# Products with their low-part passes last, joined seams, scan tables on GpSimd and grouped transposes in a neighbourhood-attention / S5 / FFN block

## The chip, the cores and the metric

One core of a Trainium2 chip runs the whole kernel. The metric is the device time of one execution in microseconds. The program is written with a tile framework whose list scheduler puts each engine's instructions into one fixed order before the run; on the chip every engine works its list off in that order, waiting on semaphores for the others.

## The reference

One layer over 2048 latent tokens (a grid 64 wide) and 256 context tokens, width 1024, all in fp32:

```
n  = modulate(rmsnorm(x)), n_ctx = modulate(rmsnorm(ctx))
q,k,v,u,gate_a,gate_s = split(n @ w_in)
a  = neighbourhood_attention(rope(q), rope(k), v, k_ctx, v_ctx, bias)
s  = glu(gelu(S5_forward(u) + S5_backward(u) + d * u))
h  = x + g1 * ((sigmoid(gate_a) * (a @ w_ba) + sigmoid(gate_s) * (s @ w_bs)) @ w_out)
h  = h + g2 * swiglu(modulate(rmsnorm(h)))     # hidden width 2816
out = rmsnorm(h)
```

S5 is a complex diagonal scan: 32 groups of 64 states in 2 directions. Here it runs over chunks of 8 tokens, 32 context chunks and 256 latent ones (288 columns).

## The kernel before

**Products.** Every dense fp32 product is made of fp32r passes. `split` (L68) makes of a tensor a high part on ScalarE (L70, `whi`) and a remainder on VectorE (L71, `wlo`). `mm3` (L89) then issues three matmuls for each 128-row slice k: high x high, and the two mixed ones. So the low part of the first slice of a weight is wanted by the second or third matmul of a product. `piece` (L79) loads 512 KB of weights over the SP queue and splits them; `cols` (L96) has the weights stationary, `rows` (L111) and the FFN's second product have them moving. `prod` (L1062) has its own copy of the three passes for the FFN's first product, a Strassen-like scheme of seven 256-column products per tile.

**Stages.** `norm_u` normalises and projects u; then `s5` and `in_proj` (the q, k, v and gate columns, four blocks of 512 tokens) are laid over each other: `in_proj` has a low priority and fills TensorE beside the scan, later beside `attention`; `merge` follows, and the FFN takes the second half of the time. The normalised tokens of a block are eight tiles `n` of a ring of twelve, reloaded from memory for blocks 1 to 3 (L357).

**The scan.** `s5` runs over 4 quarters and 2 sub-blocks (8 rounds). Each round loads u over the POOL queue into `ut` (L651), transposes it on TensorE (L658 to L661: four transposes and one ScalarE copy for each of four groups, the context chunk transposed twice because it stands at both ends of a row of `ug`), and builds small matrices. Then come four passes (2 pairs of groups x 2 directions), 32 in the kernel. A pass makes a table of complex exponentials `er`, `ei` of 288 columns by doubling (L734 to L744): copies of the first 32 columns and four rounds of two scalings on ScalarE (L741, L742) and two multiply-adds on VectorE (L743, L744), each round needing the one before. Then it multiplies the driven states `pv` (PSUM, L750) by the table (L757 to L760), scans (L762), multiplies back and writes `h` (L765 to L772). The tables have two buffers. At the start of block 1 of `in_proj`, `biases` puts the attention biases together on GpSimd (L442, L443) and stores them.

The scheduler sets the order by priorities and its own estimate of times, so a change in one stage also shifts what stands beside it.

Of the kernel before, what the change touches and what calls it, by code (L numbers as in the profile page):

```python
# [18 lines left out]
P = 128  # L19
# [33 lines left out]
class Kernel:  # L53
# [35 lines left out]
    def mm3(self, ps, l, r, first, last):  # L89

        mm = self.nc.tensor.matmul
        mm(ps, l[0], r[0], start=first, stop=False)  # L92
        mm(ps, l[0], r[1], start=False, stop=False)  # L93
        mm(ps, l[1], r[0], start=False, stop=last)  # L94

    def cols(self, pool, src, kt, c0, n, ops, tag="ps"):  # L96

        nm = 8 // kt  # L100
        for c in range(n):
            w = self.piece(src, 0, c0 + c, kt)
            for m in range(nm):
                sl = slice(m * P, (m + 1) * P)
                for i, (nt, f) in enumerate(ops):
                    ps = pool.tile([P, nt], F32, name=tag)
                    for k in range(kt):
                        self.mm3(ps, (w[0][:, k, sl], w[1][:, k, sl]), f(k), k == 0, k == kt - 1)
                    yield c * nm + m, i, ps

    def rows(self, pool, src, c, ops, tag="ps"):  # L111


        w = [self.piece(src, r, c, 4) for r in range(2)]
        for i in range(0, len(ops), 2):
            ps = pool.tile([P, 2, 256], F32, name=tag)
            for j in range(2):
                for k in range(KD):
                    self.mm3(ps[:, j], ops[i + j](k), (w[k // 4][0][:, k % 4], w[k // 4][1][:, k % 4]), k == 0, k == KD - 1)
            yield i, ps  # L120
# [163 lines left out]
    def norm_u(self, ring, s5p):  # L284

        nc, I = self.nc, self.I
        with ExitStack() as ctx:
# [19 lines left out]
            def u(ops, t0, i0, i1):  # L307
                for c in range(2):
                    for i in range(i0, i1, 2):
                        ps = pm.tile([P, 2, 256], F32, name="ps")  # L310
                        for j in range(2):
                            for k in range(KD):
                                w = wu[c * 2 + k // 4]
                                self.mm3(ps[:, j], ops[i + j](k), (w[0][:, k % 4], w[1][:, k % 4]), k == 0, k == KD - 1)
# [35 lines left out]
    def in_proj(self, ring, ev, pm, nt, nct):  # L350
        nc, I = self.nc, self.I
        V = nc.vector
        for b in range(NB):
# [16 lines left out]
            def qk(c0, ops, isk):  # L370
                for jj, i, ps in self.cols(pm, I["w_qk"], KD, c0, 4, ops):
# [50 lines left out]
            for gi in range(2):  # L422
                for m, _, ps in self.cols(pm, I["w_gate"], KD, gi * 8, 8, [lat]):
# [205 lines left out]
    def s5(self):  # L629
        nc, I = self.nc, self.I  # L630
        V = nc.vector
        with ExitStack() as ctx:
# [7 lines left out]
            for q in range(4):  # L640
                yn = [bp.tile([P, SC, 8, 16], F32, name=f"yn{cb}") for cb in range(2)]
                for sb in range(4 // NQ):
# [84 lines left out]
                    for p0 in range(0, NQ, 2):  # L727
                        hst = {}
                        for p in (p0, p0 + 1):
                            for d in range(2):  # L730
                                pr = d * 16 + pr0 + p
                                er = pp.tile([P, SEQC], F32, name="er")
                                ei = pp.tile([P, SEQC], F32, name="ei")
                                nc.scalar.copy(er[:, 0:32], self.eb[:, 0, :, pr])  # L734
                                nc.scalar.copy(ei[:, 0:32], self.eb[:, 1, :, pr])
                                for i, m in enumerate((32, 64, 128, 256)):
                                    w = min(m, SEQC - m)
                                    zr, zi, zn = (self.zz[:, i, x, pr:pr + 1] for x in range(3))
                                    ea = pp.tile([P, P], F32, name="ea", bufs=1)
                                    eb = pp.tile([P, P], F32, name="eb", bufs=1)  # L740
# [278 lines left out]
    def ffn_in(self, ch, b, X, pm, os, tp, up):  # L1019
# [77 lines left out]
    def ffn(self, xs_, os, xp, tp, pm, first):  # L1097
        nc, I = self.nc, self.I
        V = nc.vector
        with ExitStack() as ctx:  # L1100
# [13 lines left out]
            for b in range(NB):  # L1114
# [4 lines left out]
                for g, (p0, p1) in enumerate(groups):  # L1119
# [39 lines left out]
                    def product(c, m2, j, w):  # L1159
                        js = slice(j * P, (j + 1) * P)  # L1160
                        for m in range(2):
                            zh, zl = zs[m2, m]
                            self.mm3(pos[j], (zh[:, js], zl[:, js]), (w[0][:, m], w[1][:, m]), m2 == p0 and m == 0, m2 == p1 - 1 and m == 1)
# [183 lines left out]
```

## Time and profile before

| | us |
|---|---|
| median of 3 runs | 3233.86 (3228.43 to 3234.4) |
| profiled execution, device time | 3233.39 |
| its span in the profile | 3231.6 |
| TensorE matmul busy in the span | 3119.2 |
| VectorE / ScalarE / GpSimd busy | 2348.4 / 1570.3 / 898.9 |

A wait is listed under the instruction that waited and the one that released it. TensorE's instructions overlap, so the distance between starts, not the duration of one, tells what a matmul costs in a dense stretch. The granted clock is 1.00 at 2.4 GHz and 0.5 at 1.2 GHz.

### The profile page before, as it was taken

What the parts mean: (1) busy time and instruction counts of PE and PEld (TensorE: products, weight loads), DVE (VectorE), ACT (ScalarE), POOL (GpSimd) and SP (SyncE); (2) the same over time, 40 slices, a digit from 0 to 9 for tenths busy, and PEclk for the clock granted to TensorE, in tenths of its full rate; (3) what the DMA queues carried; (4) which work ended last, traced back from release to release, by engine and by line L of the source; (5) the groups of instructions that cost most, each with busy time, mean ns of one, the idle gap of its engine ahead of it and who ended that gap; (6) DMA issues with size and microseconds to landing.
All of it is one profiled execution on the core that took longest, in us unless ns stands there. A gap on an engine that the chain in (4) does not pass through costs nothing.

```text
span 3231.6 us, 54283 instructions
## 1 busy us (share of the span) xinstructions
PE 3119.2 (97%) x20600; PEld 2727.7 (84%) x20600; DVE 2348.4 (73%) x4153; ACT 1570.3 (49%) x2746; POOL 898.9 (28%) x856
## 2 busy tenths in 40 slices
PE   7999978999999998999999999999999999999998
PEld 5987766787787778788888988888989898989988
DVE  6689787897753565665657867887858966897766
ACT  4445434454355555555554444445535543554534
POOL 2000052000223232323300544742242423341243
PEclk9999989999999999999999999999999999999999
DMA  8545567454776897987847434434344434443332
GB/s 321 186 125 172 166 194 241 163 163 140 228 211 193 268 259 213 277 238 220 254 130 269 139 126 146 141 131 147 122 136 132 150 111 131 141 147 131 112 111 101
DMA packets 212853, 564.27 MB, mean 175 GB/s; under 512 B 31785, under 2 KB 63657, under 8 KB 212593
## 3 DMA queue, kind: packets, MB, share of 16 engines
q1 hardware_dynamic: 155008, 437.48, 41.2%
q0 software_dynamic: 28032, 87.64, 10.0%
q10 hardware_dynamic: 29552, 35.70, 3.2%
q8 instruction: 162, 2.65, 0.3%
q14 instruction: 99, 0.80, 0.1%
HBM read 446.95 MB, written 111.61 MB: 173 GB/s over the span
## 4 chain that ended last, share of the span: by engine, by line
PE 79%; DVE 9%; DMA 6%; issue 3%; POOL 1%; ACT 1%; SPq 0%; ACTq 0%; DVEq 0%; POOLq 0%
PE ps L92 15%; PE ps L94 15%; PE ps L93 15%; PE ps L1068 8%; PE ps L1066 8%; PE ps L1067 8%; PE o L924 3%; DVE wlo L71 3%; PE w L884 2%; PE w L905 1%; DMA raw<-in_w_qk 1%; PE pv L750 1%; PE c L886 1%; PE c L907 1%; DVE n L1130 1%
## 5 line engine op out<-in xcount | busy, mean ns | idle before, releaser
L71 DVE TENSOR_TENSOR wlo<-raw,whi 128x1024 fp32r<-128x1024 f32 (+1 forms) x522 | 688.0, 1325 | 324.6 <-ACT whi L70 323.1
L70 ACT CAST whi<-raw 128x1024 fp32r<-128x1024 f32 (+1 forms) x522 | 508.3, 976 | 519.6 <-PE ps L94 185.8
L1066 PE MATMUL ps<-X,whi 128*128 128x256 f32 x2464 | 693.4, 284 | 13.2 <-DVE u L1078 8.4
L1068 PE MATMUL ps<-X,wlo 128*128 128x256 f32 x2464 | 692.4, 284 | 11.9 <-DVE wlo L71 11.7
L1067 PE MATMUL ps<-X,whi 128*128 128x256 f32 x2464 | 689.9, 283 | 0.0
L1066 PEld LDWEIGHTS ps<-X,whi 128*128 128x128 f32 x2464 | 471.2, 191 | 17.9 <-DVE u L1078 11.7
L1068 PEld LDWEIGHTS ps<-X,wlo 128*128 128x128 f32 x2464 | 470.5, 191 | 15.1 <-DVE wlo L71 14.9
L1067 PEld LDWEIGHTS ps<-X,whi 128*128 128x128 f32 x2464 | 471.3, 191 | 0.5
L92 PE MATMUL ps<-n,whi 128*128 128x512 f32 (+1 forms) x800 | 318.2, 398 | 10.3 <-ACT t L382 6.7
L93 PE MATMUL ps<-n,whi 128*128 128x512 f32 (+1 forms) x800 | 316.7, 396 | 0.0
L94 PE MATMUL ps<-n,wlo 128*128 128x512 f32 (+1 forms) x800 | 316.3, 396 | 0.5 <-DVE wlo L71 0.5
L92 PE MATMUL ps<-whi,zh 128*128 128x512 f32 x704 | 277.1, 395 | 0.0
L94 PE MATMUL ps<-whi,zl 128*128 128x512 f32 x704 | 277.0, 394 | 0.0
L93 PE MATMUL ps<-wlo,zh 128*128 128x512 f32 x704 | 276.9, 394 | 0.0
L1049 POOL TENSOR_TENSOR os<-raw 128x512 f32<-128x512 f32 x66 | 117.4, 1780 | 406.7 <-DMA raw<-in_w_f 330.7
L70 ACT CAST whi<-os 128x1024 fp32r<-128x1024 f32 x110 | 115.5, 1050 | 204.1 <-PE ps L1067 91.7
L71 DVE TENSOR_TENSOR wlo<-os,whi 128x1024 fp32r<-128x1024 f32 x110 | 151.3, 1376 | 62.9 <-ACT whi L70 62.9
L92 PEld LDWEIGHTS ps<-n,whi 128*128 128x128 f32 x800 | 151.3, 189 | 49.6 <-ACT t L382 9.0
L93 PEld LDWEIGHTS ps<-n,whi 128*128 128x128 f32 x800 | 151.5, 189 | 35.6 <-issue 4.1
L94 PEld LDWEIGHTS ps<-n,wlo 128*128 128x128 f32 x800 | 151.3, 189 | 35.0 <-issue 1.8
L1050 POOL TENSOR_TENSOR os<-raw,os 128x512 f32<-128x512 f32 x88 | 134.0, 1523 | 150.4 <-DMA raw<-in_w_f 148.5
L92 PE MATMUL ps<-y,whi 128*128 128x512 f32 x384 | 155.5, 406 | 5.1 <-DVE t L968 1.8
(343 smaller groups left out, 7098.8 us busy)
## 6 DMA issues: line engine op xcount, KB each, us to landing
raw<-in_w_f SPq DMA_DIRECT2D x198, 512.0 KB
raw<-sums SPq DMA_DIRECT2D x66, 512.0 KB
raw<-in_w_gate SPq DMA_DIRECT2D x64, 512.0 KB
raw<-in_w_f SPq DMA_DIRECT2D x66, 256.0 KB
raw<-in_w_qk SPq DMA_DIRECT2D x32, 512.0 KB
gsc<-e ACTq DMA_DIRECT2D x64, 256.0 KB
raw<-in_w_m SPq DMA_DIRECT2D x32, 512.0 KB
t<-gsc SPq DMA_DIRECT2D x64, 256.0 KB
```

The lines of the kernel that those rows point to most:

```text
L70: self.nc.scalar.copy(hi, x)
L71: self.nc.vector.tensor_tensor(lo, x, hi.bitcast(F32), op=ALU.subtract)
L92: mm(ps, l[0], r[0], start=first, stop=False)
L93: mm(ps, l[0], r[1], start=False, stop=False)
L94: mm(ps, l[1], r[0], start=False, stop=last)
L884: nc.tensor.matmul(slv, q[:, qs], kl, start=(n == 0), stop=(n == 1))
L924: nc.tensor.matmul(o[h, g, :, hf, :], l, r, start=(n == 0), stop=(n == nb + 1), skip_group_check=True)
L1049: nc.gpsimd.tensor_tensor(s24[:, 0], s13[:, 0], a11, op=ALU.subtract)
L1050: nc.gpsimd.tensor_tensor(s24[:, 1], a12, s24[:, 0], op=ALU.subtract)
L1066: mm(dst, a[0][:, k], xh, start=(first and k == 0), stop=False, skip_group_check=True)
L1067: mm(dst, a[0][:, k], xl, start=False, stop=False, skip_group_check=True)
L1068: mm(dst, a[1][:, k], xh, start=False, stop=(k == 3), skip_group_check=True)
```

## The change

Four edits. `mm3` takes the slices of a whole product and issues the passes that need the weights' low part last (`moving` says which operand the weights are); all users of it and `prod` go through it. `cols` can join two neighbouring weight columns (`pair`): both pieces are taken first, and the product runs the first half of k for both, then the second half; this is used at the first two k columns of blocks 1 to 3 and at the last two gate columns of blocks 0 to 2. The scan's tables are made by GpSimd alone. The transposes of a round are grouped: the context chunk once for four groups, the others in twos, with three ScalarE copies instead of four.

```diff
-    def mm3(self, ps, l, r, first, last):
+    def mm3(self, ps, pairs, moving=False, first=True, last=True, **kw):
         mm = self.nc.tensor.matmul
-        mm(ps, l[0], r[0], start=first, stop=False)
-        mm(ps, l[0], r[1], start=False, stop=False)
-        mm(ps, l[1], r[0], start=False, stop=last)
+        for i, (l, r) in enumerate(pairs):
+            mm(ps, l[0], r[0], start=(first and i == 0), stop=False, **kw)
+            if moving:
+                mm(ps, l[1], r[0], start=False, stop=False, **kw)
+            else:
+                mm(ps, l[0], r[1], start=False, stop=False, **kw)
+        for i, (l, r) in enumerate(pairs):
+            a, b = (l[0], r[1]) if moving else (l[1], r[0])
+            mm(ps, a, b, start=False, stop=(last and i == len(pairs) - 1), **kw)
...
+            if pair is not None and c == pair:
+                f = ops[0][1]
+                ws = [self.piece(src, 0, c0 + c + i, kt) for i in range(2)]
+                pss = [pool.tile([P, ops[0][0]], F32, name=tag) for _ in range(2)]
+                for h in range(2):
+                    for w, ps in zip(ws, pss):
+                        ks = range(h * kt // 2, (h + 1) * kt // 2)
+                        self.mm3(ps, [((w[0][:, k], w[1][:, k]), f(k)) for k in ks], first=h == 0, last=h == 1)
...
+                    pt = psT.tile([P, NG, NCC], F32, name="pt")
                     for g in range(NG):
-                        pt = psT.tile([P, SEQC + NCC], F32, name="pt")
-                        nc.tensor.transpose(pt[:, 0:NCC], uc[:NCC, g], self.ident[:NCC, :NCC])
-                        for cb in range(2):
-                            nc.tensor.transpose(pt[:, NCC + cb * P:NCC + cb * P + P], un[cb][:, g], self.ident)
-                        nc.tensor.transpose(pt[:, SEQC:SEQC + NCC], uc[:NCC, g], self.ident[:NCC, :NCC])
-                        nc.scalar.copy(ug[:, g, :], pt)
+                        nc.tensor.transpose(pt[:, g], uc[:NCC, g], self.ident[:NCC, :NCC])
+                    ends = ug.rearrange("p g (n c) -> p g n c", c=NCC)[:, :, ::SEQC // NCC]
+                    nc.scalar.copy(ends, pt.unsqueeze(2).to_broadcast([P, NG, 2, NCC]))
+                    for g in range(0, NG, 2):
+                        pt = psT.tile([P, 2, 2, P], F32, name="pt")
+                        for j in range(2):
+                            for cb in range(2):
+                                nc.tensor.transpose(pt[:, j, cb], un[cb][:, g + j], self.ident)
+                        nc.scalar.copy(ug[:, g:g + 2, NCC:SEQC], pt.rearrange("p j c t -> p j (c t)"))
...
-                                nc.scalar.copy(er[:, 0:32], self.eb[:, 0, :, pr])
-                                nc.scalar.copy(ei[:, 0:32], self.eb[:, 1, :, pr])
+                                ee = pp.tile([P, 2, SEQC], F32, name="er")
+                                er, ei = ee[:, 0], ee[:, 1]
+                                G = nc.gpsimd
+                                G.tensor_copy(ee[:, :, 0:32], self.eb[:, :, :, pr])
                                 for i, m in enumerate((32, 64, 128, 256)):
                                     w = min(m, SEQC - m)
-                                    nc.scalar.activation(ea[:, :w], er[:, 0:w], AF.Copy, scale=zr)
-                                    nc.scalar.activation(eb[:, :w], ei[:, 0:w], AF.Copy, scale=zr)
-                                    V.scalar_tensor_tensor(er[:, m:m + w], ei[:, 0:w], zn, ea[:, :w], op0=ALU.mult, op1=ALU.add)
-                                    V.scalar_tensor_tensor(ei[:, m:m + w], er[:, 0:w], zi, eb[:, :w], op0=ALU.mult, op1=ALU.add)
+                                    zr, zi = (self.zz[:, i, x, pr:pr + 1].unsqueeze(1).to_broadcast([P, 2, w]) for x in range(2))
+                                    ea = pp.tile([P, 2, P], F32, name="ea", bufs=1)
+                                    G.tensor_tensor(ee[:, :, m:m + w], ee[:, :, 0:w], zr, op=ALU.mult)
+                                    G.tensor_tensor(ea[:, :, :w], ee[:, :, 0:w], zi, op=ALU.mult)
+                                    G.tensor_tensor(er[:, m:m + w], er[:, m:m + w], ea[:, 1, :w], op=ALU.subtract)
+                                    G.tensor_tensor(ei[:, m:m + w], ei[:, m:m + w], ea[:, 0, :w], op=ALU.add)
...
         def prod(dst, a, x, first=True):
-            for k in range(4):
-                mm = nc.tensor.matmul
-                xh, xl = X[k][:, 0, x], X[k][:, 1, x]
-                mm(dst, a[0][:, k], xh, start=(first and k == 0), stop=False, skip_group_check=True)
-                mm(dst, a[0][:, k], xl, start=False, stop=False, skip_group_check=True)
-                mm(dst, a[1][:, k], xh, start=False, stop=(k == 3), skip_group_check=True)
+            self.mm3(dst, [((a[0][:, k], a[1][:, k]), (X[k][:, 0, x], X[k][:, 1, x])) for k in range(4)], first=first, skip_group_check=True)
```

TensorE, the first product of the FFN, before (`X` are the moving tokens, `whi` and `wlo` the weights' parts):

```order
L1066 MATMUL ps<-X_17782,whi 128x256
L1067 MATMUL ps<-X_17782,whi 128x256
L1066 MATMUL ps<-X_17782,whi 128x256
L1068 MATMUL ps<-X_17782,wlo 128x256
L1066 MATMUL ps<-X_17783,whi 128x256
L1067 MATMUL ps<-X_17783,whi 128x256
L1068 MATMUL ps<-X_17783,wlo 128x256
```

The same place now:

```order
L94 MATMUL ps<-X_17542,whi 128x256
L98 MATMUL ps<-X_17542,whi 128x256
L94 MATMUL ps<-X_17543,whi 128x256
L98 MATMUL ps<-X_17543,whi 128x256
L94 MATMUL ps<-X_17544,whi 128x256
L98 MATMUL ps<-X_17544,whi 128x256
L94 MATMUL ps<-X_17545,whi 128x256
L98 MATMUL ps<-X_17545,whi 128x256
L101 MATMUL ps<-X_17542,wlo 128x256
```

The first `wlo` pass moved from the third or fourth place to the ninth.

ScalarE in the scan before, one table (`er`, `ei`, `ea`, `eb`) between copies out of PSUM (`e`) and their stores:

```order
L734 COPY er<-eb 128x32
L741 ACTIVATE ea<-er,zz 128x32
L735 COPY ei<-eb 128x32
L742 ACTIVATE eb<-ei,zz 128x32
L741 ACTIVATE ea<-er,zz 128x64
L742 ACTIVATE eb<-ei,zz 128x64
L412 COPY e<-ps 128x512
L741 ACTIVATE ea<-er,zz 128x128
L742 ACTIVATE eb<-ei,zz 128x128
```

GpSimd now, where such a table stands around the load of u (`ut`):

```order
L754 COPY er<-eb 128x2x32
L759 TENSOR_TENSOR er<-er,zz 128x2x32
L760 TENSOR_TENSOR ea<-er,zz 128x2x32
L759 TENSOR_TENSOR er<-er,zz 128x2x32
L666 DMA ut<-us 128x8x64
L761 TENSOR_TENSOR er<-er,ea 128x32
L762 TENSOR_TENSOR er<-er,ea 128x32
L759 TENSOR_TENSOR er<-er,zz 128x2x64
L760 TENSOR_TENSOR ea<-er,zz 128x2x64
L761 TENSOR_TENSOR er<-er,ea 128x64
```

The copy of `ps` on ScalarE no longer stands in the middle of a table; the load of `ut` on the POOL queue now does.

## Rows read from the trace of the kernel before

**Rows 1.** The page, busy time of each engine, share of the span, instructions.
```profile
PE 3119.2 (97%) x20600; PEld 2727.7 (84%) x20600; DVE 2348.4 (73%) x4153; ACT 1570.3 (49%) x2746; POOL 898.9 (28%) x856
```

**Rows 2.** Stretches of the scan: length, busy time of PE, PEld, DVE, ACT, POOL; clock, DMA.
```profile
180.00:400.00 220.00, 220.00 (x1281) 177.81 (x1281) 189.26 (x407) 108.27 (x241) 8.72 (x11) 1.00 0.51 158
400.00:550.00 150.00, 122.84 (x647) 98.61 (x646) 122.86 (x204) 54.92 (x110) 64.46 (x66) 0.91 0.69 213
550.00:870.00 320.00, 319.66 (x1721) 252.99 (x1720) 269.53 (x535) 152.98 (x312) 17.65 (x30) 1.00 0.52 169
180.00:870.00 690.00, 662.50 (x3645) 529.41 (x3645) 581.66 (x1144) 316.16 (x662) 90.83 (x107) 0.98 0.55 175
```

**Rows 3.** Waits of TensorE, 400 to 550 us: us in total, times, longest.
```profile
PE pv L750 <- DVE p L758: 9.0, 2, 7.2
PE ps L92 <- ACT t L382: 5.4, 2, 4.7
PE pv L750 <- ACT win L695: 4.6, 1, 4.6
```

**Rows 4.** Waits of ScalarE, 180 to 870 us.
```profile
ACT ea L741 <- DVE er L743: 77.8, 55, 3.0
...
ACT eb L742 <- DVE ei L744: 20.0, 21, 3.7
```

**Rows 5.** Waits of TensorE over the whole span.
```profile
PE ps L1068 <- DVE wlo L71: 11.7, 12, 1.7
...
PE ps L1066 <- DVE u L1078: 8.4, 11, 1.6
```

**Rows 6.** Timeline of TensorE in the FFN: start, duration in us.
```profile
2299.78 0.28 PE L1066 MATMUL ps<-X,whi 128*128 128x256 f32 x1
2299.90 0.28 PE L1067 MATMUL ps<-X,whi 128*128 128x256 f32 x1
```

**Rows 7.** Timeline of TensorE at a group's transposes in the scan.
```profile
571.64 0.24 PE L658 MATMUL pt<-ident,un 32*128 32x32 f32 x1
571.82 0.44 PE L660 MATMUL pt<-ident,un 128*128 128x128 f32 x2
```

**Rows 8.** Groups of ScalarE, 180 to 870 us: busy us, mean ns, idle before.
```profile
L741 ACT ACTIVATE ea<-er,zz 128x32 f32<-128x32 f32 (+1 forms) x125 | 43.3, 346 | 85.3 <-DVE er L743 77.8 <-DMA vs<-e 4.3 <-DVE ei L744 1.5
L742 ACT ACTIVATE eb<-ei,zz 128x32 f32<-128x32 f32 (+1 forms) x125 | 42.5, 340 | 24.7 <-DVE ei L744 20.0 <-DMA vs<-e 2.9 <-DVE p L765 0.9
...
L734 ACT COPY er<-eb 128x32 f32<-128x32 f32 x30 | 7.4, 247 | 13.8 <-DVE p L765 12.7 <-DVE ei L744 1.1
```

**Rows 9.** Groups of VectorE, 180 to 870 us.
```profile
L744 DVE SCALAR_TENSOR_TENSOR ei<-er,zz,eb 128x128 f32<-128x128 f32 (+1 forms) x126 | 37.5, 298 | 0.2
L743 DVE SCALAR_TENSOR_TENSOR er<-ei,zz,ea 128x128 f32<-128x128 f32 (+1 forms) x126 | 36.5, 290 | 1.4 <-ACT ea L741 0.4
```

**Rows 10.** Groups of GpSimd by form, 0 to 180 us.
```profile
L179 POOL COPY sel<-ident 2x2 f32<-2x2 f32 x1 | 0.2, 180 | 0.1
```

**Rows 11.** Groups of GpSimd by form, 405 to 500 us.
```profile
L442 POOL TENSOR_TENSOR n<-am,n 128x480 f32<-128x480 f32 x12 | 16.7, 1409 | 53.1 <-DMA n<-in_rpb 38.1 <-DVE wlo L71 14.9
L443 POOL TENSOR_TENSOR n<-n,am 128x480 f32<-128x480 f32 x12 | 14.2, 1190 | 0.1
```

**Rows 12.** Groups of VectorE by form, 180 to 405 us.
```profile
L71 DVE TENSOR_TENSOR wlo<-raw,whi 128x1024 fp32r<-128x1024 f32 x27 | 32.9, 1219 | 18.7 <-ACT whi L70 18.5
L772 DVE TENSOR_TENSOR h<-p,p 64x256 f32<-64x256 f32 x24 | 10.1, 420 | 0.3
...
L757 DVE TENSOR_TENSOR p<-pv,er 128x576 f32<-128x576 f32 x12 | 9.0, 753 | 0.2
```

**Rows 13.** Groups of VectorE by form, 405 to 500 us.
```profile
L71 DVE TENSOR_TENSOR wlo<-raw,whi 128x1024 fp32r<-128x1024 f32 x9 | 12.6, 1402 | 9.8 <-ACT whi L70 9.8
L772 DVE TENSOR_TENSOR h<-p,p 64x256 f32<-64x256 f32 x6 | 5.7, 948 | 0.1
...
L757 DVE TENSOR_TENSOR p<-pv,er 128x576 f32<-128x576 f32 x4 | 3.0, 751 | 0.1
```

More of the change, by code (lines that the diff above doesn't have):

```diff
@@ L87, in piece, with cols @@
         return hi, lo
-    def mm3(self, ps, l, r, first, last):
+    def mm3(self, ps, pairs, moving=False, first=True, last=True, **kw):
         mm = self.nc.tensor.matmul
-        mm(ps, l[0], r[0], start=first, stop=False)
-        mm(ps, l[0], r[1], start=False, stop=False)
-        mm(ps, l[1], r[0], start=False, stop=last)
-    def cols(self, pool, src, kt, c0, n, ops, tag="ps"):
+        for i, (l, r) in enumerate(pairs):
[7 more added lines that the diff above has]
+            mm(ps, a, b, start=False, stop=(last and i == len(pairs) - 1), **kw)
+    def cols(self, pool, src, kt, c0, n, ops, tag="ps", pair=None):
         nm = 8 // kt
         for c in range(n):
+            if pair is not None and c == pair:
[6 more added lines that the diff above has]
+                        self.mm3(ps, [((w[0][:, k], w[1][:, k]), f(k)) for k in ks], first=h == 0, last=h == 1)
+                for i, ps in enumerate(pss):
+                    yield c + i, 0, ps
+            if pair is not None and c in (pair, pair + 1):
+                continue
             w = self.piece(src, 0, c0 + c, kt)
@@ L106, in cols @@
                     ps = pool.tile([P, nt], F32, name=tag)
-                    for k in range(kt):
-                        self.mm3(ps, (w[0][:, k, sl], w[1][:, k, sl]), f(k), k == 0, k == kt - 1)
+                    self.mm3(ps, [((w[0][:, k, sl], w[1][:, k, sl]), f(k)) for k in range(kt)])
                     yield c * nm + m, i, ps
@@ L117, in rows @@
             for j in range(2):
-                for k in range(KD):
-                    self.mm3(ps[:, j], ops[i + j](k), (w[k // 4][0][:, k % 4], w[k // 4][1][:, k % 4]), k == 0, k == KD - 1)
+                self.mm3(ps[:, j], [(ops[i + j](k), (w[k // 4][0][:, k % 4], w[k // 4][1][:, k % 4])) for k in range(KD)], True)
             yield i, ps
@@ L311, in u @@
                         for j in range(2):
-                            for k in range(KD):
-                                w = wu[c * 2 + k // 4]
-                                self.mm3(ps[:, j], ops[i + j](k), (w[0][:, k % 4], w[1][:, k % 4]), k == 0, k == KD - 1)
+                            self.mm3(ps[:, j], [(ops[i + j](k), tuple(x[:, k % 4] for x in wu[c * 2 + k // 4])) for k in range(KD)], True)
                         e = ep.tile([P, 2, 256], F32, name="e")
@@ L370, in qk @@
             def qk(c0, ops, isk):
-                for jj, i, ps in self.cols(pm, I["w_qk"], KD, c0, 4, ops):
+                for jj, i, ps in self.cols(pm, I["w_qk"], KD, c0, 4, ops, pair=0 if b and isk else None):
                     with self.hot():
@@ L422, in in_proj @@
             for gi in range(2):
-                for m, _, ps in self.cols(pm, I["w_gate"], KD, gi * 8, 8, [lat]):
+                for m, _, ps in self.cols(pm, I["w_gate"], KD, gi * 8, 8, [lat], pair=6 if gi and b < NB - 1 else None):
                     g = ev.tile([P, TB], F32, name="e")
@@ L1160, in product @@
                         js = slice(j * P, (j + 1) * P)
-                        for m in range(2):
-                            zh, zl = zs[m2, m]
-                            self.mm3(pos[j], (zh[:, js], zl[:, js]), (w[0][:, m], w[1][:, m]), m2 == p0 and m == 0, m2 == p1 - 1 and m == 1)
+                        zw = [(tuple(z[:, js] for z in zs[m2, m]), (w[0][:, m], w[1][:, m])) for m in range(2)]
+                        self.mm3(pos[j], zw, True, m2 == p0, m2 == p1 - 1)
                     for c in range(2):
```

5 lines of the change are left out of this document (removed).

## The prediction, made before the run

> **What bounds the kernel now.** I read the page first: TensorE is busy for 3119.2 of 3231.6 us [rows 1]. So the edits can gain only what TensorE loses (112.4 us of idle in that count, and stretches at the lower clock) and what they take off its own work. The split by stretches says where the loss lies: in the scan, from 180 to 870 us, TensorE is idle for 27.5 us, and nearly all of it (150.0 - 122.84 = 27.2) falls between 400 and 550 us, where the granted clock is 0.91 as well, which is worth 0.09 x 150 = 13.5 us of full clock [rows 2]. Before and after that stretch TensorE has no gap that counts. The waits of TensorE name the reasons in the stretch: VectorE reading `pv` (9.0 us), and ScalarE's copies out of PSUM (5.4 and 4.6 us) [rows 3]. The waits of ScalarE say what it does there: it stands 77.8 + 20.0 = 97.8 us in the scan until VectorE has done a step of a table [rows 4], and every copy out of PSUM queued behind such a step stands with it. For the second half of the kernel the waits over the whole span give the low parts of weights (11.7 us in 12 waits) and `u` (8.4 us in 11), both VectorE being late [rows 5].
>
> **Low part last.** The edit removes and adds no matmul. In the dense FFN a 256-column matmul starts 2299.90 - 2299.78 = 0.12 us after the one before, although it follows on the same weights [rows 6]; each pass has its own weight load before and after, so I price the regrouping itself at nothing. What moves is the need: the first `wlo` pass of a product is the ninth matmul instead of the third, 6 x 0.12 = 0.72 us later. Twelve waits x 0.72 = 8.6 us, of 11.7 at most [rows 5]. VectorE is still late, though, so some of this returns as waits for `u`: I take 7 us, between 0 and 11.7. The high part of a moving weight's second piece is wanted four matmuls earlier (0.5 us); it is cast by ScalarE ahead of time, and only the first products of a stage would feel it.
>
> **Grouped transposes.** Of 8 rounds x 4 groups x 2 transposes of the context chunk half go: 32. The next instruction starts 571.82 - 571.64 = 0.18 us after such a transpose [rows 7]: 32 x 0.18 = 5.8 us, in stretches where TensorE is full, so it counts. If the remaining ones take a little longer in a row of four, less: 5 us, between 2 and 6. ScalarE's copies fall from 32 to 24 with more columns each; off the path.
>
> **Seams.** A joined pair wants both weight pieces at once and lets go of the first half of the tokens earlier. No wait of TensorE for reloaded tokens stands among its waits in the scan [rows 3], and the scheduler already lays scan work over the seam. I take 0, between -5 (a seam in the lossy stretch eased) and +5 (the third weight piece loaded late, since the pair holds two of three buffers).
>
> **Tables on GpSimd.** Removed: on ScalarE 43.3 + 42.5 + 2 x 7.4 = 100.6 us (the second copy, L735, is like L734) [rows 8], on VectorE 37.5 + 36.5 = 74.0 us [rows 9], and the to and fro between them. Added: 32 tables x (1 copy + 16 operations) on GpSimd. Columns of a table: 64 copied, 2 x 512 scaled, 2 x 256 combined, 1600 in all. By the nearest row, 1190 ns for 480 columns [rows 11], that is 2.5 ns each, 4.0 us; with a fixed part for each instruction as large as the smallest copy, 180 ns [rows 10], 17 x 0.18 = 3.1 us more. So 4.0 to 7.1 us a table; I take the upper, 32 x 7.1 = 227 us in a scan of 690 us, 33% of GpSimd. A pass comes every 690 / 32 = 21.6 us and there are two table buffers, so the making is hidden behind the pass before.
>
> What it does to VectorE is the open point. Between 405 and 500 us GpSimd spends 16.7 + 14.2 = 30.9 us on the biases [rows 11], a third of that stretch too, and there VectorE's operations with both inputs in SBUF are longer: `h` 948 instead of 420 ns (+126%), `wlo` 1402 instead of 1219 (+15%), while the product that reads PSUM stays at 751 against 753 [rows 12, 13]. The scan holds 581.7 us of VectorE work [rows 2], 507.7 without the tables. Bounds: 0 if the short GpSimd operations slip between, and as for both rows together, (9 x 183 + 6 x 528) ns = 4.8 us on 9 x 1.219 + 6 x 0.420 = 13.5 us, 36%, so 183 us. I take the row that weighs most, `wlo`: 15% x 507.7 = 76 us. That eats the 74.0 us removed: VectorE stays as full as it is.
> The Trainium skill (SBUF — State Buffer, Who interferes with whom) speaks against the edit: a VectorE instruction with two SBUF inputs and a GpSimd instruction that reads SBUF exclude each other, the later one blocking for the whole instruction. These rows agree in kind, PSUM readers included. By that rule, if every GpSimd microsecond blocked VectorE, the stage would have 227 - 74 = 153 us more of VectorE, which I call an estimate and an extreme; the third rival below stands on the rows alone.
>
> So VectorE gains nothing and ScalarE loses 100.6 us of work and 97.8 us of standing. Of TensorE's 27.2 us in the lossy stretch, the ScalarE waits (10.0) should go, and some of the VectorE wait (9.0), because the weights are cast and the rotary chain starts sooner; but the biases keep GpSimd there. I take half, 13.6 us, between 40.7 (all idle and the clock) and a loss of as much. The low clock I leave out. What is late next is VectorE. Loads of `ut` now queue behind table steps on the POOL queue, and a step that waits for a free table buffer holds them; they were issued up to a round ahead, so I count nothing, but it is a way into the third rival.
>
> **Sum.** 3233.4 (profiled execution) - 7 - 5 - 0 - 13.6 = 3207.8. The profiled execution stands 0.5 us under the median of the runs, so I predict 3208 us, 0.8% faster. With 0 to 11.7, 2 to 6, +-5 for the seams, and 5 to 22 for the tables, its own range is about 3192 to 3226.
>
> **Rivals.** *The waits only change their place (chance 0.16).* VectorE is what is late: the low part's wait becomes one for `u` [rows 5], and in the scan the tables' 74 us come back as blocked time while TensorE waits for `pv` as now. Then only the transposes count: 3228.4, no change by the measure of 0.2% (6.5 us, about what can be told here). For it: 8.4 us of waits for `u` at the same places. Against it: ScalarE's 97.8 us of standing are real and go.
> *The lossy stretch closes altogether (0.14).* If TensorE starves there because ScalarE is held by table steps, 27.2 + 13.5 us come back with the 12 of the other edits: 3233.4 - 40.7 - 12 = 3180.7. For it: nothing else in the scan loses time. Against: GpSimd is busy for 64.5 of these 150 us already [rows 2], and the biases stay.
> *GpSimd blocks VectorE (0.23).* From the point at which VectorE loses more than the removed 74.0 us and its slack of 690 - 581.7 = 108 us together, 182 us or 0.8 us for each of the 227 us of tables, the scan goes at VectorE's pace; the upper bound above, 183 us, lies just there, and locally, in the biases' stretch, it is reached sooner. The stretch that loses would be twice as long: another 27.2 us of idle and 13.5 of clock, less 5 for the transposes: 3233.4 + 35.7 = 3269. For it: the lossy stretch is the one in which GpSimd computes. Against: in it ScalarE and the stores are late as well, and `wlo`, the largest group, suffers least.
>
> **How the numbers follow.** Forecast 0.47, rivals 0.16, 0.14 and 0.23. The forecast and the second rival are faster: 0.61; the first is no change: 0.16; the third slower: 0.23. The range reaches from 3176, just under the second rival, to 3262, which leaves out the worse half of the third.
>
> **What would show it.** The low part: the waits of TensorE for `wlo` in the FFN fall from 11.7 to under 4 us, and those for `u` don't grow by as much. Transposes: 32 fewer, as many of 128 columns. Tables: no ScalarE wait for table steps, ScalarE busy about 100 us less, GpSimd about 230 us more in the scan, `h` and `wlo` of VectorE longer throughout the scan and its whole busy time there near 580 us. TensorE's idle time between 400 and 550 us is halved. Wrong would be: gaps before `pv` with VectorE as releaser all over the scan (third rival), a scan that ends later than 870 us, or table operations much longer than 0.4 us on average, with `ut` arriving late.

## The result and the profile after

The changed kernel takes 3244.81 us (median of 5 runs, 3243.49 to 3252.89), the kernel before 3233.86 us beside it: a ratio of 1.0054, 95% interval [1.0037, 1.0070]. It is slower by 0.5%, where 0.8% faster was predicted. Its profiled execution took 3244.1 us, with a span of 3242.3.

First the page, as in [rows 1]: busy time, share and instructions of each engine.

```profile
PE 3110.7 (96%) x20568; PEld 2724.4 (84%) x20568; DVE 2340.6 (72%) x3897; ACT 1492.2 (46%) x2418; POOL 1187.5 (37%) x1400
```

TensorE's busy time fell by 8.5 us and its 32 transposes are gone, but its idle time rose from 112.4 to 3242.3 - 3110.7 = 131.6 us: 19.2 more idle less 8.5 of work is the 10.7 us by which the span grew. Next the stretches of the scan, as in [rows 2]: length, busy time of PE, PEld, DVE, ACT, POOL; clock, DMA.

```profile
180.00:400.00 220.00, 209.20 (x1233) 170.38 (x1234) 192.93 (x315) 76.98 (x117) 125.59 (x227) 0.98 0.47 144
400.00:550.00 150.00, 119.56 (x646) 98.81 (x646) 110.34 (x151) 38.76 (x57) 96.74 (x133) 0.90 0.66 203
550.00:870.00 320.00, 308.08 (x1653) 243.56 (x1652) 264.40 (x419) 118.68 (x169) 165.41 (x292) 0.99 0.56 178
180.00:870.00 690.00, 636.83 (x3529) 512.75 (x3530) 567.68 (x883) 234.42 (x342) 387.74 (x650) 0.97 0.55 173
```

The stretch that lost time before loses as much as ever (30.4 us idle against 27.2), and the two that lost nothing now lose 10.8 and 11.9 us. ScalarE gave up 81.7 us, GpSimd took on 296.9. VectorE's busy time fell by only 14.0 us, although instructions of 74.0 us went: some of these had overlapped their neighbours (in the trace of before the others alone cover 537.9 us of the 581.7), and the others became longer. The scan itself ends earlier, at 847.3 us instead of 860.5 (its last product `py`), but from there to the first product of the FFN it is 964.7 us instead of 941.9, and so the FFN starts 9.6 us later, at 1812.0 instead of 1802.4 us. Who makes TensorE wait there (waits of TensorE from 180 us to the scan's end at 847, as in [rows 3]; us in total, times, longest):

```profile
PE py L800 <- DVE h L790: 22.8, 9, 11.5
PE pv L768 <- DVE p L776: 14.6, 2, 11.6
PE ps L94 <- DVE qt L392: 4.8, 1, 4.8
```

VectorE is named, but it waits itself. The same stretch for VectorE, and then for GpSimd:

```profile
DVE p L775 <- POOL er L761: 19.9, 6, 7.9
```
```profile
POOL er L754 <- DVE p L784: 105.2, 13, 21.4
POOL n L457 <- DMA n<-in_rpb: 51.8, 8, 14.1
```

VectorE waits for tables. GpSimd, at other times, is ahead and waits for VectorE to give one of the two table buffers back; and it waits for the loads of the biases. One gap shows what makes a table late (timelines of TensorE, VectorE and GpSimd; start, duration, engine, line, tiles, in brackets the idle time before):

```profile
482.65 2.19 PE L768 MATMUL pv<-ug,win 128*64 128x288 f32 x8 [11.59 <-DVE p L776]
```
```profile
472.24 1.23 DVE L71 TENSOR_TENSOR wlo<-raw,whi 128x1024 fp32r<-128x1024 f32 x1 [9.01 <-ACT whi L70]
481.17 0.76 DVE L775 TENSOR_TENSOR p<-pv,er 128x576 f32<-128x576 f32 x1 [7.71 <-POOL er L761]
481.85 0.75 DVE L776 TENSOR_TENSOR p<-pv,er 128x576 f32<-128x576 f32 x1
```
```profile
443.49 0.31 POOL L754 COPY er<-eb 128x64 f32<-128x64 f32 x1
453.19 2.58 POOL L457 TENSOR_TENSOR n<-am,n 128x480 f32<-128x480 f32 x2 [9.39 <-DMA n<-in_rpb]
...
468.05 2.38 POOL L457 TENSOR_TENSOR n<-am,n 128x480 f32<-128x480 f32 x2 [4.04 <-DMA n<-in_rpb]
...
470.76 0.39 POOL L760 TENSOR_TENSOR ea<-er,zz 128x128 f32<-128x128 f32 x1
471.10 0.28 POOL L754 COPY er<-eb 128x64 f32<-128x64 f32 x1
471.35 2.96 POOL L458 TENSOR_TENSOR n<-n,am 128x480 f32<-128x480 f32 x2
474.26 1.48 POOL L460 DMA_DIRECT2D be<-n  x2
475.73 0.73 POOL L451 DMA_DIRECT2D n<-in_rpb  x1
476.48 0.33 POOL L761 TENSOR_TENSOR er<-er,ea 128x64 f32<-128x64 f32 x1
...
480.89 0.25 POOL L761 TENSOR_TENSOR er<-er,ea 128x32 f32<-128x32 f32 x1
481.10 0.25 POOL L762 TENSOR_TENSOR er<-er,ea 128x32 f32<-128x32 f32 x1
```

TensorE has stood since 471 us. VectorE has nothing else to do and waits 7.71 us for a table. This table was begun at 443.49 us and is done 37.9 us later, because its steps stand on GpSimd's queue between the sums of the biases: the queue stops for 9.39 and 4.04 us until a load of the biases lands, and at the end 5.1 us of bias sums and DMA issues (471.35 to 476.48) cut the steps in two. The next two tables, made among the biases as well, take 44.4 and 49.4 us from first copy to last step; elsewhere in the scan nearly all take 10 to 14. VectorE's waits for the first two of these three are 7.7 and 7.9 us, most of the 19.9. What the operations of a table cost (GpSimd by form, 180 to 847 us; busy us, mean ns):

```profile
L760 POOL TENSOR_TENSOR ea<-er,zz 128x256 f32<-128x256 f32 x32 | 31.9, 998 | 0.0
L760 POOL TENSOR_TENSOR ea<-er,zz 128x64 f32<-128x64 f32 x63 | 30.5, 484 | 2.4
L762 POOL TENSOR_TENSOR er<-er,ea 128x32 f32<-128x32 f32 x63 | 27.8, 442 | 0.0
```

With the other forms of this view the 17 means add up to 9.6 us a table, where 4.0 to 7.1 was the estimate. Beside them VectorE's instructions that have both inputs in SBUF are longer, those that read PSUM are not (VectorE by form, 180 to 870 us; compare [rows 12, 13]):

```profile
L71 DVE TENSOR_TENSOR wlo<-raw,whi 128x1024 fp32r<-128x1024 f32 x84 | 111.5, 1328 | 27.8 <-ACT whi L70 25.4 <-issue 1.9
L780 DVE TENSOR_TENSOR_SCAN v<-r,v 128x288 f32<-128x288 f32 x64 | 53.9, 872 | 0.1
L789 DVE TENSOR_TENSOR h<-p,p 64x256 f32<-64x256 f32 x64 | 32.9, 514 | 1.6
...
L784 DVE TENSOR_TENSOR p<-v,er 128x512 f32<-128x512 f32 x32 | 26.4, 824 | 0.0
...
L775 DVE TENSOR_TENSOR p<-pv,er 128x576 f32<-128x576 f32 x32 | 24.2, 756 | 26.9 <-POOL er L761 19.9 <-PE pv L768 5.3
```

In the same view of the kernel before, `wlo` took 1254 ns, the scan 746, `h` 495, the product `p` from `v` 686, and the product from PSUM 753. Over all forms (each form's count here times the growth of its mean) the lengthening adds up to 44 us.

In the FFN little moved. 1420 us of it hold 1394.48 us of TensorE work after and 1394.92 before; the waits, as in [rows 5], are fewer and longer for `wlo`:

```profile
PE ps L101 <- DVE wlo L71: 14.3, 7, 3.4
PE ps L94 <- DVE u L1091: 8.9, 11, 1.8
```

And a round's transposes (timeline of TensorE, beside [rows 7]):

```profile
194.79 0.43 PE L673 MATMUL pt<-ident,un 32*128 32x32 f32 x4
195.15 1.09 PE L680 MATMUL pt<-ident,un 128*128 128x128 f32 x8
196.00 0.97 PE L101 MATMUL ps<-n,wlo 128*128 128x512 f32 x3
```

A whole round takes 196.00 - 194.79 = 1.21 us. Before, one of its four groups took 0.72 us (from 571.64 to the next product, which starts at 572.36), a round up to 2.88. Added up over the eight rounds, from each first transpose to the next other product, it was 21.9 us and is 9.7 without waits: 12 us less work.

### The profile page after: what moved, and what is told of

It is laid out like the page before. It is cut to its first block, busy times and chain, and to the rows that moved or that the text cites. A ratio compares the mean times of both kernels' runs of the same rounds, so it can differ in the third digit from the quotient of the medians.

```text
span 3242.3 us, 54137 instructions
## 1 busy us (share of the span) xinstructions
PE 3110.7 (96%) x20568; PEld 2724.4 (84%) x20568; DVE 2340.6 (72%) x3897; ACT 1492.2 (46%) x2418; POOL 1187.5 (37%) x1400
## 3 DMA queue, kind: packets, MB, share of 16 engines
q1 hardware_dynamic: 155008, 437.48, 40.7%
## 4 chain that ended last, share of the span: by engine, by line
PE 69%; DVE 13%; DMA 9%; POOL 3%; issue 3%; ACT 1%; SPq 0%; DVEq 0%; POOLq 0%; ACTq 0%
PE ps L94 20%; PE ps L101 20%; PE ps L98 13%; PE ps L96 7%; DVE wlo L71 3%; PE o L942 3%; DMA n<-in_rpb 2%; PE w L902 1%; PE w L923 1%; DMA raw<-in_w_m 1%; DMA raw<-in_w_out 1%; PE c L904 1%; PE c L925 1%; DVE v L780 1%; DMA raw<-in_w_vu 1%
## 5 line engine op out<-in xcount | busy, mean ns | idle before, releaser
L94 PE MATMUL ps<-X,whi 128*128 128x256 f32 x2464 | 620.6, 284 | 11.2 <-DVE u L1091 8.9
L98 PE MATMUL ps<-X,whi 128*128 128x256 f32 x2464 | 618.6, 283 | 0.0
L101 PE MATMUL ps<-X,wlo 128*128 128x256 f32 x2464 | 399.1, 285 | 14.3 <-DVE wlo L71 14.3
L101 PEld LDWEIGHTS ps<-X,wlo 128*128 128x128 f32 x2464 | 341.8, 193 | 16.0 <-DVE wlo L71 15.9
L101 PE MATMUL ps<-wlo,zh 128*128 128x512 f32 x704 | 221.1, 394 | 0.0
L101 PE MATMUL ps<-n,wlo 128*128 128x512 f32 (+1 forms) x800 | 209.2, 394 | 0.0
L94 PEld LDWEIGHTS ps<-n,whi 128*128 128x128 f32 x800 | 152.1, 190 | 49.3 <-issue 5.8
L914 ACT ACTIVATE s<-s,mn 128x696 f32<-128x696 f32 (+1 forms) x128 | 108.5, 848 | 114.0 <-DVE s L913 109.7
```

Of the source, the lines that this page charges most:

```text
L94: mm(ps, l[0], r[0], start=(first and i == 0), stop=False, **kw)
L98: mm(ps, l[0], r[1], start=False, stop=False, **kw)
L101: mm(ps, a, b, start=False, stop=(last and i == len(pairs) - 1), **kw)
L914: nc.scalar.activation(s[:, :nk + LC], s[:, :nk + LC], AF.Exp, scale=-1.0, bias=mn[:, 1:2], accum_out=mn[:, 2:3])
```

## The experiments

All times are medians beside runs of the kernel before on the same chip; a ratio is to those runs, with its 95% interval. The expectations name theories by letters. In A the tables on GpSimd cost the time; in B, mostly, the new order of the passes; in C the scheduler draws a new instruction order ahead of the FFN for an edit, and that drawing moves the time by more than the edits do; in D, at the end, the edits themselves cost the 11 us, the tables above all. A "drawing" is one such order.

**One part of the change at a time.** Tables back on ScalarE and VectorE, all else as changed:

```diff
-G.tensor_tensor(ee[:, :, m:m + w], ee[:, :, 0:w], zr, op=ALU.mult)
...
+nc.scalar.activation(ea[:, :w], er[:, 0:w], AF.Copy, scale=zr)
...
+V.scalar_tensor_tensor(er[:, m:m + w], ei[:, 0:w], zn, ea[:, :w], op0=ALU.mult, op1=ALU.add)
```


> The changed kernel with the scan's tables made by ScalarE and VectorE again (the other three edits kept). Theory A (the GpSimd tables cost the time: a table takes about 9 us there, can start only when its buffer is free, so VectorE waits for it in a burst of passes and TensorE for VectorE): 3218 to 3232 us, under the kernel before by the transposes and a part of the low-part waits. Rival B (the new pass order and the shifted static order cost the time): stays at 3240 to 3250 us. Either way the waits of TensorE for wlo in the FFN should stay near 14 us, since the tables lie in another stage.


Measured: 3252.24 us, 1.0062 [1.0040, 1.0083]. Without the tables on GpSimd it is no faster, though VectorE's operations are about as short as in the kernel before (scan 760 ns, `wlo` 1242; over all forms the lengthening is under 1 us). So the lengthening comes from the tables on GpSimd, and the time does not follow it.

The reverse, the kernel before with only the tables on GpSimd:

> The kernel before with only the tables moved to GpSimd. Theory A: 3245 to 3260 us, VectorE waiting about 20 us for table steps and TensorE over 25 us for VectorE's h and p in the scan. Rival B (pass order is the cause): 3228 to 3238 us.


Measured: 3271.03 us, 1.0123 [1.0099, 1.0146]. That is slower than any theory expected. So the same edit costs 1.2% alone, and on top of the rest it makes no difference that can be told (1.0054 with it, 1.0062 without): the parts don't add.

The kernel before with only the low part last, everywhere; then with it in the FFN alone, where the order of everything ahead stays word for word:

```diff
-mm(ps, l[1], r[0], start=False, stop=last)
+for i, (l, r) in enumerate(pairs):
+    a, b = (l[0], r[1]) if moving else (l[1], r[0])
+    mm(ps, a, b, start=False, stop=(last and i == len(pairs) - 1), **kw)
```


> The kernel before with only the new order of the passes (no joined pairs, old tables, old transposes). Theory A: 3222 to 3235 us. Rival B: 3240 us or more. A third theory C (the static order is so tight that any edit shifts it by 10 us in either direction): this one and the run with the tables back differ by over 8 us without a wait that names the edit.

> The kernel before with the new pass order in the FFN's two products alone; everything ahead of the FFN keeps its order of instructions. Theory C (the low part last neither costs nor gains by itself; what cost 39 us in the run with the pass order alone was the new static order ahead of the FFN): within 4 us of the kernel before, FFN stage 1429 us +-3, the waits for wlo about as long as now (12 to 16 us). My prediction's step: 7 us faster. Rival B (the pass order itself slows the dense products): slower by 5 us or more, since over half of the matmuls stand there.


Measured: 3269.22 us, 1.0111 [1.0087, 1.0136], and 3233.15 us, 1.0001 [0.9989, 1.0012]. In the FFN the edit does nothing: its waits there read

```profile
PE ps L108 <- DVE wlo L71: 13.7, 8, 3.4
PE ps L101 <- DVE u L1087: 8.5, 10, 1.8
```

against 11.7 in 12 and 8.4 in 11 [rows 5]: the waits for `wlo` are fewer and longer. What the first run lost arises ahead of the FFN: its FFN starts 36.0 us later than before (1838.4 against 1802.4 us) and takes 1430.8 us against 1429.2.

The kernel before with only the grouped transposes:

> The kernel before with only the grouped transposes. By the prediction's term alone: 3226 to 3230 us (5 us less TensorE work where it is full). Theory C: the 5 us are there in TensorE's busy time (about 6 us less), but the time lands anywhere in 3220 to 3270, by the waits of the new order between 860 and 1840 us.


Measured: 3230.03 us, 0.9995 [0.9984, 1.0006]. The work is gone (TensorE is busy for 3104.9 us instead of 3119.2) but not seen in the time: TensorE's idle time from 180 to 1800 us rises from 59.8 to 73.1 us, by about as much.

The changed kernel without the joined pairs:

```diff
...
-self.cols(pm, I["w_gate"], KD, gi * 8, 8, [lat], pair=6 if gi and b < NB - 1 else None)
+self.cols(pm, I["w_gate"], KD, gi * 8, 8, [lat])
```


> The changed kernel without the joined pairs. If the seams gain what they are meant to: slower than the changed kernel by up to 5 us, with waits of TensorE for reloaded tokens at the seams. Theory C: anywhere in 3225 to 3270 us, most of the difference behind the scan.


Measured: 3288.88 us, 1.0166 [1.0144, 1.0187], the slowest of all runs.

**The tables' price.** The changed kernel with one table made, 31 left out; and with three table buffers (for the space, `y2` shares `p2`'s buffer and there is one `strip`):

```diff
+if q == 0 and sb == 0 and p == 0 and d == 0:
     G.tensor_copy(ee[:, :, 0:32], self.eb[:, :, :, pr])
...
-ee = pp.tile([P, 2, SEQC], F32, name="er")
+ee = pp.tile([P, 2, SEQC], F32, name="er", bufs=3)
```


> The changed kernel with one table made by GpSimd and used by all 32 passes (31 tables are left out, so the scan's values differ). Theory A: the waits for tables and most of the waits of TensorE for h go; 3200 to 3220 us, which is also the most that any way of making the tables can give. Rival B: 3238 us or more, since the tables are not what costs.

> The changed kernel with three table buffers instead of two (room made by letting the gelu's scratch share a buffer and by one strip buffer). Theory A (a table starts only when a buffer comes free, so a burst of passes is paced by GpSimd): VectorE's wait for table steps in the scan falls from 27 to under 10 us and GpSimd's wait for the release (105 us) to under 60. Rival (the shared port slows both engines): these waits stay, and VectorE's scan at 288 columns stays at 0.87 us instead of 0.75. The whole time may move by 20 us either way with the order, so the waits decide here.


Measured: 3226.58 us, 0.9988 [0.9973, 1.0004], which is between the two expectations, and 3233.06 us, 1.0002 [0.9991, 1.0013]. Without tables the scan ends at 794 us instead of 847, yet the whole is only about 20 us shorter (0.9988 against 1.0054): from the scan's end to the FFN's start it is 1010 us instead of 965, so work that lay beside the scan comes after it. With a third buffer VectorE waits less for tables (19.9 us before):

```profile
DVE p L775 <- POOL er L761: 7.5, 1, 7.5
```

and the time is 12 us shorter, although the scan's operations are as long as in the changed kernel (907 ns against 872). GpSimd's wait for a free buffer, expected under 60 us, is still 97.7. What the third buffer takes away is the waiting for a table, not the lengthening: one table more is done before the biases begin, and of those made among them only one is waited for long. It redraws the order too, so the 12 us are not its own for certain.

**Redrawing with the same work.** First the kernel before with the four passes of a row-block pair in another order, and the same on top of the transposes:

```diff
-for p in (p0, p0 + 1):
-    for d in range(2):
+for p, d in ((p0, 0), (p0 + 1, 0), (p0, 1), (p0 + 1, 1)):
```


> The kernel before with the four passes of a pair of groups in another order (both pairs forward, then both backward): the same work, the same instructions on each engine, the same buffers. Theory C (the static order ahead of the FFN decides by tens of us): differs from the kernel before by more than 7 us, most likely slower, with the FFN's length unchanged at 1429 us. Rival: within 6 us, since no work changed; then the losses of the four edits have to be found in their own waits.

> The kernel before with the grouped transposes and the other order of the four passes. Adding up the two single runs: 3230 + 10 = 3240 us. Theory C: the two do not add, anywhere in 3215 to 3255 us, with TensorE's busy time again about 12 us lower by the transposes.


Measured: 3243.12 us, 1.0033 [1.0020, 1.0046], and 3248.88 us, 1.0045 [1.0029, 1.0061].

Then the changed kernel with a 4-column memset on GpSimd in each pass, which changes the order on all engines, and, as a control, with one in each round, which leaves the order on TensorE, VectorE, ScalarE and SP as it was:

```diff
+nz = pp.tile([P, 4], F32, name="nz", bufs=1)
+nc.gpsimd.memset(nz, 0.0)
```


> The changed kernel with one more GpSimd memset of 4 columns (about 0.1 us) in each of the 32 passes, which nothing waits for; it only makes the scheduler choose another order. Theory C: differs from the changed kernel (3244.8) by more than 7 us in either direction, anywhere in 3225 to 3270. Rival: 3240 to 3250 us.

> Control for the run with a memset in each pass: the changed kernel with one GpSimd memset of 4 columns in each of the 8 rounds. Here the order of instructions on TensorE, VectorE, ScalarE and the SP queue stays word for word that of the changed kernel. Theory C (the order decides, the memset costs nothing): 3240 to 3250 us, like the changed kernel. Rival (the extra GpSimd instructions cost): 3250 us or more.


Measured: 3266.60 us, 1.0101 [1.0083, 1.0119], and 3245.45 us, 1.0042 [1.0028, 1.0056]. Against the changed kernel's 1.0054 the first is slower by 0.5%, the second is the same. The added work can't be the cause: a memset takes 0.1 us, 32 of them 3.2 us on GpSimd.

So the one comparison of before and after could be a comparison of two drawings. Six runs tested this: both kernels, redrawn in the same three ways: directions exchanged, row blocks exchanged, and both, as here:

```diff
-for p in (p0, p0 + 1):
-    for d in range(2):
+for p in (p0 + 1, p0):
+    for d in (1, 0):
```


> The kernel before with the two directions of each row block taken in the other order: the same instructions in the same number, another drawing of the order ahead of the FFN. Theory C (the drawing of the order alone moves the time by 10 to 45 us, and the changed kernel's 11 us are no more than such a draw): it differs from the kernel before by more than 6.5 us, to 3243-3275. Rival D (the 11 us are the work of the change itself, above all of the tables on GpSimd; redrawing is worth little): within 6.5 us of the kernel before, 3227-3240.

> The kernel before with the two row blocks of a pair taken in the other order: the same work, another drawing. C: differs from the kernel before by more than 6.5 us, 3243-3275, and from the kernel with the directions exchanged as well. D: within 6.5 us, 3227-3240.

> The kernel before with both the directions and the row blocks of a pair exchanged: the same work, a fourth drawing. C: again more than 6.5 us over the kernel before, 3243-3270 on its 3233. D: 3227-3240.

> The changed kernel with the two directions of each row block taken in the other order: the same work as the changed kernel. C: anywhere between 3230 and 3270, and the mean of the changed kernel's drawings lies within the spread of the drawings of the kernel before. D: 3238-3251, and the mean of the changed kernel's drawings lies about 11 us above that of the kernel before.

> The changed kernel with the two row blocks of a pair taken in the other order. C: anywhere between 3230 and 3270. D: 3238-3251.

> The changed kernel with both exchanged. C: within 10 us of the kernel before with the same two exchanges, on either side of it, as the two pairs so far (0.04% and 0.11% apart). D: 11 us (0.34%) above it.

Measured, with TensorE's idle time (length of the stretch less its busy time) in two stretches of the windows view:

| drawing | before: us, ratio | after: us, ratio | idle 180-870 us, before / after | idle 870-1800 us, before / after |
|---|---|---|---|---|
| as written | 3233.9, 1 | 3244.8, 1.0054 [1.0037, 1.0070] | 27.5 / 53.2 | 32.3 / 25.7 |
| directions | 3254.5, 1.0065 [1.0043, 1.0087] | 3253.6, 1.0069 [1.0045, 1.0094] | 37.1 / 49.3 | 43.2 / 38.6 |
| row blocks | 3258.2, 1.0081 [1.0053, 1.0110] | 3260.4, 1.0092 [1.0059, 1.0124] | 35.3 / 50.6 | 54.9 / 37.0 |
| both | 3251.6, 1.0065 [1.0049, 1.0080] | 3250.8, 1.0059 [1.0043, 1.0076] | 30.7 / 55.5 | 43.9 / 25.8 |

The three redrawn pairs differ by +0.04, +0.11 and -0.06%, by 0.03% in the mean, with some 0.2% of uncertainty (from the six intervals). With the same exchange in both, then, the change neither costs nor gains anything that can be told. The kernel before, as written, is simply the best of the five orders of the same work that were run, by 0.3 to 0.8%, and most edits ahead of the FFN give that up (the transposes alone and the changed kernel with three buffers did not). The rival's expectation, 11 us (0.34%) above before, fell in the mean of the pairs. Pairing by exchange is a choice, since no two kernels share an order. Taken as two families of five, with the swap of passes for before and the memset in each pass for after, the mean ratios are 1.0049 and 1.0075, and single drawings scatter by 0.2 to 0.3%: a loss of some tenths of a percent isn't excluded, the forecast gain of 0.8% is.

The table also shows what the change does in every drawing: more idle time in the scan (52.2 against 32.7 us in the mean of four) and less behind it (31.8 against 43.6). The waits of TensorE from 180 to 870 us tell a part of why in the scan. Before with both exchanged, then after with both exchanged:

```profile
PE ps L92 <- ACT t L382: 16.7, 3, 10.0
PE ps L92 <- ACT e L412: 4.0, 1, 4.0
PE ps L92 <- DMA n<-ns: 3.5, 1, 3.5
PE pv L750 <- DVE p L758: 2.9, 1, 2.9
```
```profile
PE pv L768 <- DVE p L776: 18.6, 1, 18.6
PE py L799 <- DVE h L790: 12.5, 7, 3.5
PE ps L94 <- ACT e L441: 6.1, 2, 4.7
PE ps L94 <- DVE qt L392: 4.8, 1, 4.8
```

Before, the longest wait is for another thing in each drawing (as written 7.2 us for VectorE's `p`, with the directions exchanged 15.8 for ScalarE's `e`, with the row blocks 10.8 for a cast weight, with both 10.0 for `t`). After, the largest sums are always VectorE's `p` and `h`, and the long ones among them stand behind a table: VectorE's waits for tables from 180 to 870 us are 19.9, 21.6, 26.6 and 30.0 us in the four drawings, and 15.6, 18.4, 23.0 and 27.7 of them are for two tables made among the biases. With both exchanged:

```profile
DVE p L775 <- POOL er L761: 30.0, 5, 24.1
```

That part belongs to the change. But the tables are not all of the added idle time: TensorE's idle time from 180 to 870 us is 41.8 us in the run with the tables back, 44.5 with the transposes alone and 36.7 with the tables alone, one drawing each.

## Why the prediction was wrong

**Its base.** The sum took the profiled execution and corrected it, as if all that no term spoke of stayed as it was; "Before and after that stretch TensorE has no gap that counts" was read as a property of the kernel. It is one of its drawing: with the same work TensorE's idle time from 180 to 1800 us goes from 59.8 us to 74.6 to 90.2. This decided the sign. It is not the whole miss: with the same exchange in both kernels the difference is 0.03%, where the terms promised 0.8%. No term for it stood in the sum or among the rivals, though the order of the changed kernel was there to be seen and differs ahead of the FFN all along.

**Tables on GpSimd (-13.6).** The term with the wrong sign in its own stretch; what the tables are worth in the whole time stays open, since every run with or without them has another order. ScalarE's waits for table steps went, as said, and its busy time fell by 82 us (predicted 100.6). But the idle time from 400 to 550 us was not halved, it rose by 3.2 us, and 22.7 us came in the rest of the stretch to 870 us, where it was 0.3. The step that failed is "A pass comes every 690 / 32 = 21.6 us and there are two table buffers, so the making is hidden behind the pass before". It took averages. Outside the biases' stretch (422 to 547 us) passes come in fours, 8 to 17 us apart, with 29 to 67 us between the fours, but that cost little: there no pass waits longer than 2 us for its table. The making is not hidden where GpSimd also sums the biases: there a table takes 38 to 49 us instead of 10 to 14, because its steps queue behind sums, DMA issues and waits for loads. The prediction had read that the biases keep GpSimd there and halved the gain for it; that the steps of a table would queue behind them it did not count. A table's operations cost 9.6 us, against 7.1 taken. The lengthening of VectorE was sized too large: 76 us predicted, 44 measured; but of the 74.0 us taken off VectorE only 43.8 had been time of its own, since the table steps overlap their neighbours. By the Trainium skill (SBUF — State Buffer, Who interferes with whom) a VectorE instruction with two SBUF inputs contends with a GpSimd instruction that reads SBUF. The trace agrees in kind, SBUF readers longer and PSUM readers not, but 296.9 us more of GpSimd lengthened VectorE's instructions by 44 us, about a seventh, not the whole.

**Low part last (-7).** Worth 0: the same FFN to about a microsecond (1430.3 us after, 1429.2 before), and the run with this edit in the FFN alone at 1.0001. The step that failed is "Twelve waits x 0.72 = 8.6 us", which takes VectorE to be late by a fixed amount, so that a later need shortens each wait: the waits became 7 instead of 12 and twice as long in the mean. So the splits must end later against TensorE's stream; what delays them was not tried.

**Transposes (-5).** The work was mis-sized: 12 us of TensorE's went. I counted the instructions that go and expected those that stay to be slower in a row; in a row they are faster. The step that failed is "in stretches where TensorE is full, so it counts": with the transposes alone the time stayed (0.9995 [0.9984, 1.0006]), and the work that went came back as 13.3 us of idle time ahead of the FFN.

**Seams (0).** Open. Without the pairs the changed kernel takes 1.0166, 0.65% more than its slowest drawing (1.0101), so more than the drawings run here explain; and the two runs with a part of the change and without pairs (tables only, order only) are slow as well. That pairs pay back what new pass order and tables cost, in the idle time behind the scan, would fit, but was not shown: only one drawing without them was timed. One sign is small: TensorE's waits for reloaded tokens (`n` from memory) are 9.3 us with the order alone and 7.8 without the pairs, none in the kernel before and 1.3 in the changed one; but with a memset in each pass, pairs in place, they are 13.0.

**The rivals.** The first said no change, which is what the redrawn pairs show, but not by its way: the waits for `wlo` did not become waits for `u`. The second fell, the lossy stretch did not close. What was named for the third, gaps before `pv` with VectorE as releaser all over the scan, is there only in part: the two waits of `pv` end at 445 and 483 us, among the biases, and elsewhere in the scan there are only short ones for `h`, of 2 us and less. Its cause, VectorE blocked by GpSimd, is the smaller one, since VectorE's busy time fell and a third buffer took waiting away without shortening its operations. Its size, +35.7, was too large for the whole because more idle time in the scan is followed by less behind it. Of the signs of being wrong, table operations longer than 0.4 us came (9.6 us over 17 is 0.57); a later end of the scan did not.

**The range.** The bounds named in the sum add up to 3188.7 and 3231.4 us, not to 3192 and 3226, and the tables, first put between 40.7 us gained and a loss of as much, enter them as 5 to 22 gained without a reason. The sum had no room for the tables to lose, which in their stretch they did.

## What to carry to other kernels

Where a scheduler sets the order, redraw both kernels in a few ways that keep the work the same, and compare the families; a single pair told 0.5% here where three more told nothing. A term read off one trace is worth only what stays when the order moves: gaps that look closed or open don't, and even 12 us of work that went came back as idle time in the one order timed. Work given to an idle engine is hidden only if its buffers cover the longest stretch in which that engine does something else or stands waiting for a load, not the average one.

## What the runs showed of the hardware

- Transposes on TensorE cost less in a row: the next instruction starts 0.36 us after the first of four of 32 columns, and 0.85 us after the first of eight of 128, about 0.1 us each (194.79 us, above); in groups of one, two and one they took 0.18 us each [rows 7].
- Short GpSimd operations have a large fixed part: with VectorE idle 32 columns take 0.25 us (481 us, above) and 256 columns 0.62 (at 478.31 and 478.88 us), so about 0.2 us is fixed, an estimate from these two. In the mean of the scan they take 0.42 to 0.44 and 0.83 to 1.0.
- A single VectorE operation can take twice its time beside a GpSimd one. In the changed kernel's timeline the product `p` takes 1.68 us, against 0.82 in the mean there and 0.69 in the kernel before, beside a bias sum that started 0.52 us ahead of it:

```profile
526.74 1.65 POOL L457 TENSOR_TENSOR n<-am,n 128x480 f32<-128x480 f32 x1
527.26 1.68 DVE L784 TENSOR_TENSOR p<-v,er 128x512 f32<-128x512 f32 x1
```
